# Sample attention by both key heads in one pass, sample state products of both halves side by side, small products queued behind the latest large one

## The chip, the cores and the metric

The kernel runs on one core of one Trainium2 chip. The metric is the time of one execution in device microseconds (us); before the change the median of three runs is 1966.09 us (1965.5 to 1967.4). PE is TensorE, DVE is VectorE, ACT is ScalarE, POOL is GpSimd, and SP is the engine whose queue issues nearly all DMA transfers here.

## The reference, cut to what matters

One decoder layer is applied to a prompt of 1024 tokens and to 8 running sequences with 8 new tokens each (64 sample tokens).

```python
x = x + 0.5 * rms_norm(swiglu(rms_norm(x, g1), ffn1_gu, ffn1_down), p1)
z = rms_norm(x, gm) @ w_in + b_in            # q, k, v | hq, hf, hi, hg
a = window_attention(q, k, v, sinks)         # prompt: 128-wide band; sample: 128 cached keys + 8 new ones
S, o = hgrn2(silu(hq), 1 - f, log f, hi, s0) # chunkwise; the sample starts from a given state
x = x + rms_norm(concat(rms_norm(a), gate(o)) @ w_out, pm)
x = x + 0.5 * rms_norm(swiglu(rms_norm(x, g2), ffn2_gu, ffn2_down), p2)
```

The sample attention has 2 key heads with 4 query heads each. For one sequence and one key head there are 32 query rows (4 heads by 8 tokens) against 136 keys. The sample recurrence has 4 heads; for each of the 8 sequences a state of 128x128 gets `S = decay * S + k^T v` over 8 tokens, and the output uses the old state.

## The kernel before, in words

All numbers are fp32. The large products are made of three fp32r products each: operands are split into a high part (ACT, L235) and a rest (DVE, L236), and `mm3` (L256) issues high by high, high by rest, rest by high (L258, L259, L260) into one PSUM bank. The tokens are three column groups of 320, 384 and 384: group 0 holds 256 prompt tokens and the 64 sample tokens, groups 1 and 2 hold prompt tokens. The program is the first FFN, the mixing part (projection `w_in_units`, attention, recurrence, projection `w_out_units`) and the second FFN. The down product of the first FFN for groups 1 and 2 is done in parts called `pair`, numbered by product: the parts 5, 3, 7 and 4 run after the projection of group 0 and before that of group 1. In a part each step takes two row blocks of the weight: the weight is loaded into `raw` (3 buffers), split into two of 8 `wsp` buffers, and the activations are loaded into `ar` (L927) and split into two halves of one `h` buffer; both share a ring of 8 buffers, from which the input of the next projection also takes its tiles. Three PSUM banks of a ring of four (`mm`) are added up by such a part, and `put` (L936) adds each to its sum with a DVE addition (L940).

The attention and the recurrence are small products that fill in. They are written as generators; `tick()` (L128) is called after every half or whole step of a large product and lets the generators advance at a rate (`pace`, L109) that is worked out from the steps still left (the second number in `ready`, L1469) and the tick at which they are due (`DUE`). The order on each engine is then set by the framework's scheduler, which may issue an instruction ahead of others that are written earlier if it thinks it is ready sooner. The small products use a second ring of four PSUM banks (`ax`).

The sample attention (`sample_attn`, L1344) goes over two halves `hb` of four sequences, and in each over the two key heads `g`: four score products (`ssc`, L1374) with 64 rows of the array and 32 columns each, mask and row maximum (DVE), exponential (ACT), two transposes (`spT`, L1391 and L1392), eight value products (`spv`, L1399 and L1403), scaling (DVE), store. There are four such rounds, one after another. The sample recurrence (`sample_hgrn`, L1418) goes over four heads `a`: value products `sav` (L1441, L1445) from the old state; the state is multiplied by its decay (POOL, L1447); then for each half `hf` of the sequences one state product `su` (L1451) with 32 rows of the array and 512 columns, and its addition to the state (DVE, L1453); the state is stored.

Of the kernel before, what the change touches and what calls it, by code (L numbers as in the profile page):

```python
# [14 lines left out]
ALU = mybir.AluOpType  # L15
# [3 lines left out]
P = 128  # L19
# [25 lines left out]
def tile_step(ctx: ExitStack, tc: tile.TileContext, A: dict, O: dict):  # L45
    nc = tc.nc
    V, S, G, PE = nc.vector, nc.scalar, nc.gpsimd, nc.tensor
# [15 lines left out]
    def axbank(s="ax"):  # L63
        return ps.tile([P, 512], F32, tag="ax", bufs=4, name=uid(s))
# [191 lines left out]
    def mm3(out, a, b, first, last, resume=False):  # L256

        PE.matmul(out, a[0], b[0], start=first, stop=False, skip_group_check=resume)  # L258
        PE.matmul(out, a[0], b[1], start=False, stop=False, skip_group_check=resume)  # L259
        return PE.matmul(out, a[1], b[0], start=False, stop=last, skip_group_check=resume)  # L260

    def hcol(h, k, w):
        return h[0][k // 4][:, k % 4, :w], h[1][k // 4][:, k % 4, :w]
# [740 lines left out]
    def mixing(tp, h):  # L1004
        w_in = A["w_in"]

        def t2(shape=(P, 512)):
            return tmp2("t2", shape)
# [335 lines left out]
        def sample_attn():  # L1344
            n = 0
            zq, kx, vn = Z[n]["q"], KX[n], VN[n]

            def cached(src, hb):
                t = tmp2("kv", (P, 4, P))
                nc.sync.dma_start(t, A[src][0, 4 * hb:4 * hb + 4].rearrange("b w g d -> w b (g d)"))  # L1350
# [12 lines left out]
            V.tensor_copy(keys[:, :, P:], kx[:, P + 256:P + 320].rearrange("p (b t) -> p b t", b=8))  # L1363
            qs = t2((P, 8, 4, 8))
            V.tensor_copy(qs.rearrange("p b m t -> p m b t"),
                          zq[:, :, 256:320].rearrange("p m (b t) -> p m b t", b=8))
            yield
            osc = dr.tile([4, P, 64], F32, name="osc")
            for hb in range(2):
                vc = cached("cache_v_win", hb)  # L1370
                for g in range(2):
                    bank = axbank("ssc")
                    for i in range(4):
                        PE.matmul(bank[32 * i:32 * i + 32, :136],  # L1374
                                  qs[64 * g:64 * g + 64, 4 * hb + i].rearrange("p m t -> p (m t)"),
                                  keys[64 * g:64 * g + 64, 4 * hb + i], start=True, stop=True)
                    p = t2((P, 136))
                    sm = small()
                    V.tensor_tensor_reduce(out=p, in0=bank[:, :136], in1=smask, op0=ALU.add, op1=ALU.max,
                                           scale=1.0, scalar=NEG, accum_out=sm[:, 0, 0:1])  # L1380
# [9 lines left out]
                    bank = axbank("spT")  # L1390
                    PE.transpose(bank[:, :P], p[:, :P], ident)  # L1391
                    PE.transpose(bank[:8, P:2 * P], p[:, P:136], ident)  # L1392
                    pT = t2((P, 2, P))
                    V.tensor_copy(pT[:, 0], bank[:, :P])
                    V.tensor_copy(pT[:8, 1], bank[:8, P:2 * P])
                    yield
                    ob = axbank("spv")
                    for i in range(4):
                        PE.matmul(ob[32 * i:32 * i + 32, :64], pT[:, 0, 32 * i:32 * i + 32],  # L1399
                                  vc[:, i, g * 64:g * 64 + 64], start=True, stop=False, skip_group_check=True)  # L1400
                    for i in range(4):
                        c = i * P + g * 64
                        PE.matmul(ob[32 * i:32 * i + 32, :64], pT[:8, 1, 32 * i:32 * i + 32],  # L1403
                                  vnb[hb][:8, c:c + 64], start=False, stop=True, skip_group_check=True)
                    o = t2((P, 64))
                    V.tensor_scalar(o, ob[:, :64], sm[:, 1, 2:3], None, op0=ALU.mult)
                    nc.sync.dma_start(osc[2 * g + hb], o)
                    yield
            o = t2()
            for b in range(8):  # L1410
                for g in range(2):
                    nc.sync.dma_start(
                        o[8 * b:8 * b + 8].rearrange("t (m g d) -> t g m d", m=4, g=2)[:, g],
                        osc[2 * g + b // 4, 32 * (b % 4):32 * (b % 4) + 32].rearrange("(m t) d -> t m d", m=4))
            yield
            yield from finish_attn(n, o, NS, slice(256, 320))

        def sample_hgrn():  # L1418
# [10 lines left out]
            for a in range(4):  # L1429
                st = big(F32, (P, 8, P))  # L1430
                nc.sync.dma_start(st, A["state_hgrn"][0][:, a].rearrange("b k v -> k b v"))
                qm = t2((P, 2, 4, 32))
                G.tensor_tensor(qm, Q[:, a, :r].rearrange("p (f t) -> p f t", f=2).unsqueeze(2).to_broadcast(
                    [P, 2, 4, 32]), own.unsqueeze(1).to_broadcast([P, 2, 4, 32]), op=ALU.mult)
                vb = t2((P, 4, P))
                V.tensor_tensor(vb[:r], z["v"][:r, 2, a * P:(a + 1) * P].unsqueeze(1).to_broadcast([r, 4, P]),
                                seqm.unsqueeze(2).to_broadcast([r, 4, P]), op=ALU.mult)
                yield
                sr = [slice(32 * hf, 32 * hf + 32) for hf in range(2)]
                for hf in range(2):  # L1440
                    PE.matmul(ob[sr[hf], a * P:(a + 1) * P], At[:r, a, sr[hf]], z["v"][:r, 2, a * P:(a + 1) * P],  # L1441
                              start=True, stop=False, skip_group_check=True)
                for b in range(4):
                    for hf in range(2):
                        PE.matmul(ob[sr[hf], a * P:(a + 1) * P], qm[:, hf, b], st[:, 4 * hf + b], start=False,  # L1445
                                  stop=b == 3, skip_group_check=True)
                G.tensor_tensor(st, st, D[:, a].unsqueeze(2).to_broadcast([P, 8, P]), op=ALU.mult)  # L1447
                yield
                for hf in range(2):
                    ub = axbank("su").rearrange("p (b t) -> p b t", b=4)  # L1450
                    PE.matmul(ub, kn[sr[hf], a], vb[sr[hf]], start=True, stop=True)  # L1451
# [318 lines left out]
```

## Time and profile before

| what | value |
|---|---|
| median of 3 runs | 1966.09 us (1965.5 to 1967.4) |
| the profiled execution, its own time | 1964.23 us |
| its span, first to last instruction | 1962.5 us |
| around the span | 1.7 us |
| PE / weight loads / DVE / ACT / POOL busy | 1944.9 / 1828.4 / 1368.5 / 932.2 / 209.1 us |
| granted PE clock, mean | 0.999 |
| DMA | 358.20 MB, 183 GB/s in the mean |

A row of the timeline gives the start of a group of instructions, its duration, engine, line, operation, the written and read tiles with the shape, and how many there are. Matmuls are pipelined, so that their durations overlap: what one costs is read from the starts of the instructions around it. An fp32 product that is not fp32r is run as two passes and counts as two in the trace. In a row of windows each engine has its busy time in that stretch, then the granted clock, the share of the DMA engines and the traffic.

### The profile page before, as it was taken

The numbers are of one execution on the slowest core, as the hardware profiler recorded it, in microseconds if no ns is written. First come the engines' busy times: TensorE is split into PE (matmuls) and PEld (weight loads), VectorE is DVE, ScalarE is ACT, GpSimd is POOL, SyncE is SP. The second block draws the span as 40 slices with busy tenths as digits, with TensorE's granted clock in tenths as the row PEclk, the third lists the DMA queues.
The fourth block names the chain that finished last, engine by engine and source line by source line (L and its number), as shares of the span: only waits on it lengthen the run. The fifth ranks groups of instructions, "written<-read, shape, count | busy, mean of one in ns | idle before, by whom it ended". The sixth has DMA issues, their size and how long they took to land.

```text
span 1962.5 us, 34190 instructions
## 1 busy us (share of the span) xinstructions
PE 1944.9 (99%) x13469; PEld 1828.4 (93%) x13469; DVE 1368.5 (70%) x2211; ACT 932.2 (48%) x1630; POOL 209.1 (11%) x213
## 2 busy tenths in 40 slices
PE   9999999999999999999999999999999999999998
PEld 8999999999998987788899898999999999999887
DVE  6976667777558666866667666745987877655666
ACT  6543333444455544744444565655544444444453
POOL 0000000000004012111232224001000000000202
PEclk9999999999999999999999999999999999999999
DMA  7543345556767645764434343556565545677874
GB/s 238 164 151 145 128 170 172 188 185 216 243 215 229 186 130 174 229 207 130 142 116 152 97 126 105 171 167 199 165 208 192 211 171 192 212 236 227 306 262 142
DMA packets 160396, 358.20 MB, mean 183 GB/s; under 512 B 16284, under 2 KB 59996, under 8 KB 160220
## 3 DMA queue, kind: packets, MB, share of 16 engines
q1 hardware_dynamic: 159228, 354.19, 54.5%
q8 instruction: 105, 1.72, 0.4%
q10 hardware_dynamic: 1008, 1.84, 0.3%
q14 instruction: 55, 0.45, 0.1%
HBM read 279.33 MB, written 77.63 MB: 182 GB/s over the span
## 4 chain that ended last, share of the span: by engine, by line
PE 94%; DVE 2%; DMA 2%; ACT 1%; issue 1%; POOL 0%; SPq 0%; DVEq 0%; POOLq 0%; ACTq 0%
PE mm L258 28%; PE mm L260 28%; PE mm L259 28%; DMA ar<-fa 1%; PE c L260 1%; PE c L258 1%; PE c L259 1%; PE sc L1154 1%; PE pv L1195 1%; PE lv L1228 1%; PE pT L1180 1%; DVE w L236 0%; PE mm L551 0%; PE av L1329 0%; DMA big<-in_x1T_dram 0%
## 5 line engine op out<-in xcount | busy, mean ns | idle before, releaser
L258 PE MATMUL mm<-h,wsph 128*128 128x320 f32 (+1 forms) x1296 | 416.3, 322 | 2.6 <-DVE sg L664 2.6
L259 PE MATMUL mm<-h,wsph 128*128 128x320 f32 (+1 forms) x1296 | 410.3, 317 | 0.0
L260 PE MATMUL mm<-h,wspl 128*128 128x320 f32 (+1 forms) x1296 | 408.9, 317 | 0.0
L236 DVE TENSOR_TENSOR wspl<-raw,wsph 128x1024 fp32r<-128x1024 f32 x200 | 250.7, 1254 | 148.9 <-ACT wsph L235 143.6
L235 ACT CAST wsph<-raw 128x1024 fp32r<-128x1024 f32 x200 | 208.9, 1047 | 296.0 <-PE mm L259 239.8
L235 ACT CAST w<-raw 128x512 fp32r<-128x512 f32 (+1 forms) x226 | 169.5, 754 | 239.7 <-PE mm L259 112.6
L236 DVE TENSOR_TENSOR w<-raw,w 128x512 fp32r<-128x512 f32 (+1 forms) x226 | 196.9, 875 | 85.4 <-ACT w L235 85.3
L258 PEld LDWEIGHTS mm<-h,wsph 128*128 128x128 f32 x1296 | 243.8, 188 | 10.2 <-issue 7.8
L259 PEld LDWEIGHTS mm<-h,wsph 128*128 128x128 f32 x1296 | 244.0, 188 | 1.7 <-issue 0.8
L260 PEld LDWEIGHTS mm<-h,wspl 128*128 128x128 f32 x1296 | 243.6, 188 | 1.4 <-issue 1.0
L258 PE MATMUL mm<-h,w 128*128 128x384 f32 x704 | 235.6, 335 | 0.0
L259 PE MATMUL mm<-h,w 128*128 128x384 f32 x704 | 235.6, 335 | 0.0
L260 PE MATMUL mm<-h,w 128*128 128x384 f32 x704 | 230.6, 335 | 0.0
L258 PE MATMUL mm<-w,h 128*128 128x512 f32 x462 | 181.5, 396 | 1.8 <-DVE big L940 1.3
L259 PE MATMUL mm<-w,h 128*128 128x512 f32 x462 | 180.3, 391 | 0.0
L260 PE MATMUL mm<-w,h 128*128 128x512 f32 x462 | 178.9, 391 | 0.4 <-DVE h L236 0.4
L229 POOL TENSOR_TENSOR sm<-sm,mhalf 128x3 f32<-128x3 f32 (+4 forms) x37 | 36.4, 987 | 1193.5 <-DVE sm L313 501.7
L258 PEld LDWEIGHTS mm<-h,w 128*128 128x128 f32 x704 | 132.2, 188 | 0.2 <-ACT big L754 0.2
L259 PEld LDWEIGHTS mm<-h,w 128*128 128x128 f32 x704 | 132.1, 188 | 0.0
L260 PEld LDWEIGHTS mm<-h,w 128*128 128x128 f32 x704 | 131.7, 188 | 0.0
L235 ACT CAST w<-t 128x512 fp32r<-128x512 f32 x176 | 106.8, 621 | 49.2 <-PE mm L260 46.0
L236 DVE TENSOR_TENSOR w<-t,w 128x512 fp32r<-128x512 f32 x176 | 119.0, 687 | 10.4 <-ACT w L235 10.4
(343 smaller groups left out, 3691.6 us busy)
## 6 DMA issues: line engine op xcount, KB each, us to landing
raw<-in_ffn_w_gu_dram SPq DMA_DIRECT2D x154, 512.0 KB
raw<-in_ffn_w_down_dram SPq DMA_DIRECT2D x74, 512.0 KB
raw<-in_w_in_dram SPq DMA_DIRECT2D x54, 512.0 KB
ar<-fa SPq DMA_DIRECT2D x70, 384.0 KB
big<-in_ffn_w_down_dram SPq DMA_DIRECT2D x88, 256.0 KB
fb<-big SPq DMA_DIRECT2D x44, 512.0 KB
raw<-fb SPq DMA_DIRECT2D x40, 512.0 KB
fa<-big SPq DMA_DIRECT2D x22, 768.0 KB
```

The lines of the kernel that those rows point to most:

```text
L229: G.tensor_tensor(y, x, mhalf[:y.shape[0], :y.shape[1]], op=ALU.pow)
L235: S.copy(hi, src)
L236: return (lo_eng or V).tensor_tensor(lo, src, hi.bitcast(F32), op=ALU.subtract)
L258: PE.matmul(out, a[0], b[0], start=first, stop=False, skip_group_check=resume)
L259: PE.matmul(out, a[0], b[1], start=False, stop=False, skip_group_check=resume)
L260: return PE.matmul(out, a[1], b[0], start=False, stop=last, skip_group_check=resume)
L1154: PE.matmul(banks[g][:, i * 256:i * 256 + wk], zq[64 * g:64 * g + 64, 2 * pr + i, b * P:(b + 1) * P], kx[64 * g:64 * g + 64, k0:k0 + wk], ...
L1180: PE.transpose(bank[:, (i * nk + kb) * P:(i * nk + kb + 1) * P], pt[g][:, i, kb * P:(kb + 1) * P], ident)
L1195: PE.matmul(ob[q0:q0 + 64, c:c + 64], pT[g][:, k1:k1 + 64], vn[:, vb, g * 64:g * 64 + 64], start=kb == 0, stop=kb == nk - 1)
L1228: PE.matmul(b4[ps_, j, a], x[:, a, cs], y[:, a, cs], start=True, stop=True)
```

## The change

There are three edits. In the sample attention both key heads are done in one round: the eight score products of a half are issued together (key head 1 first, key head 0 queued behind it on PE), both softmaxes follow, then the four transposes into one bank with two copies instead of four, then the sixteen value products into one bank, two scalings and two stores. In the sample recurrence both state products of a head are issued ahead of its value products (half 1 first, half 0 queued behind it), into two banks that are taken before; the additions to the state stay behind the decay. Last, what a `tick()` issues on PE is queued behind the large product that was written last, by an order constraint on PE alone which waits for nothing to finish. The numbers of steps in `ready` follow the generators: 11 for 17 and 10 for 14.

```diff
     def tick():
+        with tc.issue_after(latest[0].ins):
+            turn()
+
+    def turn():
         pace()
...
-        return PE.matmul(out, a[1], b[0], start=False, stop=last, skip_group_check=resume)
+        r = latest[0] = PE.matmul(out, a[1], b[0], start=False, stop=last, skip_group_check=resume)
+        return r
...
+                banks = [axbank("ssc") for _ in range(2)]
+                for g in (1, 0):
+                    with tc.issue_after(last) if g == 0 else nullcontext():
+                        for i in range(4):
+                            last = PE.matmul(banks[g][32 * i:32 * i + 32, :136],
+                                             qs[64 * g:64 * g + 64, 4 * hb + i].rearrange("p m t -> p (m t)"),
+                                             keys[64 * g:64 * g + 64, 4 * hb + i], start=True, stop=True).ins
...
+                ubs = [axbank("su").rearrange("p (b t) -> p b t", b=4) for _ in range(2)]
+                for hf in (1, 0):
+                    with tc.issue_after(last) if hf == 0 else nullcontext():
+                        last = PE.matmul(ubs[hf], kn[sr[hf], a], vb[sr[hf]], start=True, stop=True).ins
...
-                yield
                 for hf in range(2):
-                    ub = axbank("su").rearrange("p (b t) -> p b t", b=4)
-                    PE.matmul(ub, kn[sr[hf], a], vb[sr[hf]], start=True, stop=True)
                     sl = st[:, 4 * hf:4 * hf + 4]
-                    V.tensor_tensor(sl, sl, ub, op=ALU.add)
+                    V.tensor_tensor(sl, sl, ubs[hf], op=ALU.add)
...
-                    gens += [(sample_attn(), 17), (kv_out(0), 1)]
+                    gens += [(sample_attn(), 11), (kv_out(0), 1)]
...
-                    gens.append((sample_hgrn(), 14))
+                    gens.append((sample_hgrn(), 10))
```

The edits move instructions in the whole mixing part. On PE, before, in the projection of group 1, the two state products of the second head (`su`) come after two transposes of the sample attention (`spT`) and rows of the large product (`mm`), one row of which stands between the two:

```order
L1391 MATMUL spT_8898<-ident,t_1253_8796 128x128
L1392 MATMUL spT_8898<-ident,t_1253_8796 8x128
L258 MATMUL mm_8967<-h_8115,wsph_8963 128x384
L259 MATMUL mm_8967<-h_8117,wsph_8963 128x384
L1451 MATMUL su_8904<-t_1229_8697,m_1187_8458 128x512
L260 MATMUL mm_8967<-h_8115,wspl_8964 128x384
L1451 MATMUL su_8907<-t_1229_8697,m_1187_8458 128x512
```

The same engine after the change, at the third head, whose products stand as those of the fourth do:

```order
L264 MATMUL mm_9069<-h_8067,wspl_9066 128x384
L1459 MATMUL su_9119<-t_1288_9048,m_1207_8609 128x512
L1459 MATMUL su_9118<-t_1288_9048,m_1207_8609 128x512
L1461 MATMUL sav_8611<-big_6777,big_6474 32x128 x2
L1465 MATMUL sav_8611<-big_9044,t_1287_9046 32x128 x8
L262 MATMUL mm_9142<-h_8066,wsph_9138 128x384
```

The two state products of a head stand together, with the value products (`sav`) behind them. So it is at the third and the fourth head; at the first head the two stand together but apart from the value products, and at the second head one row of a large product still stands between them. In all, PE's order has 145 runs of small products between large ones, 164 before.

On SP, before, in the last part of the down product (product 4): loads of weights (`raw<-fb`) and of activations (`ar<-fa`) for its steps, loads for the next projection (`raw<-in_w_in_dram`), and two loads for the sample (`kv`, `big<-in_state_hgrn_dram`):

```order
L1350 DMA kv_8377<-in_cache_v_win_dram 128x4x128
L1431 DMA big_8461<-in_state_hgrn_dram 128x8x128
L915 DMA raw_8250<-fb_102 128x2x512
L915 DMA raw_8305<-fb_102 128x512
L927 DMA ar_8142<-fa_101 128x2x384
L242 DMA raw_8410<-in_w_in_dram 128x1024
L927 DMA ar_8207<-fa_101 128x2x384
```

The same place after the change, where ar_8093 holds the activations of the second step as ar_8142 does above:

```order
L922 DMA raw_8167<-fb_102 128x2x512
L391 DMA gb_8130<-in_norm_ffn_post_dram 128x512
L922 DMA raw_8210<-fb_102 128x2x512
L922 DMA raw_8259<-fb_102 128x512
L246 DMA raw_8366<-in_w_in_dram 128x1024
L934 DMA ar_8093<-fa_101 128x2x384
L246 DMA raw_8405<-in_w_in_dram 128x1024
```

The sample's two loads have gone from here to a later place, in the projection of group 1, and the first load for that projection now stands ahead of the activations of the second step, not behind them.

More of the change, by code (lines that the diff above doesn't have):

```diff
@@ L259, in mm3 @@
         PE.matmul(out, a[0], b[1], start=False, stop=False, skip_group_check=resume)
-        return PE.matmul(out, a[1], b[0], start=False, stop=last, skip_group_check=resume)
+        r = latest[0] = PE.matmul(out, a[1], b[0], start=False, stop=last, skip_group_check=resume)
+        return r
+    latest = [None]
     def hcol(h, k, w):
@@ L1370, in sample_attn @@
                 vc = cached("cache_v_win", hb)
-                for g in range(2):
[L1372 to L1376, printed above, removed]
+                banks = [axbank("ssc") for _ in range(2)]
[5 more added lines that the diff above has]
+                                             keys[64 * g:64 * g + 64, 4 * hb + i], start=True, stop=True).ins
+                ps_, sms = [], []
+                for g in range(2):
                     p = t2((P, 136))
                     sm = small()
-                    V.tensor_tensor_reduce(out=p, in0=bank[:, :136], in1=smask, op0=ALU.add, op1=ALU.max,
+                    V.tensor_tensor_reduce(out=p, in0=banks[g][:, :136], in1=smask, op0=ALU.add, op1=ALU.max,
                                            scale=1.0, scalar=NEG, accum_out=sm[:, 0, 0:1])
@@ L1388, in sample_attn @@
                     V.reciprocal(sm[:, 1, 2:3], sm[:, 1, 1:2])
-                    yield
[L1390 to L1397, printed above, removed]
+                    ps_.append(p)
+                    sms.append(sm)
+                yield
+                bank = axbank("spT")
+                for g in range(2):
+                    PE.transpose(bank[:, 2 * g * P:(2 * g + 1) * P], ps_[g][:, :P], ident)
+                    PE.transpose(bank[:8, (2 * g + 1) * P:(2 * g + 2) * P], ps_[g][:, P:136], ident)
+                pT = t2((P, 2, 2, P))
+                bank = bank.rearrange("p (g j t) -> p g j t", g=2, j=2)
+                V.tensor_copy(pT[:, :, 0], bank[:, :, 0])
+                V.tensor_copy(pT[:8, :, 1], bank[:8, :, 1])
+                yield
+                ob = axbank("spv")
+                for g in range(2):
                     for i in range(4):
-                        PE.matmul(ob[32 * i:32 * i + 32, :64], pT[:, 0, 32 * i:32 * i + 32],
+                        PE.matmul(ob[32 * i:32 * i + 32, g * 64:g * 64 + 64], pT[:, g, 0, 32 * i:32 * i + 32],
                                   vc[:, i, g * 64:g * 64 + 64], start=True, stop=False, skip_group_check=True)
@@ L1402, in sample_attn @@
                         c = i * P + g * 64
-                        PE.matmul(ob[32 * i:32 * i + 32, :64], pT[:8, 1, 32 * i:32 * i + 32],
+                        PE.matmul(ob[32 * i:32 * i + 32, g * 64:g * 64 + 64], pT[:8, g, 1, 32 * i:32 * i + 32],
                                   vnb[hb][:8, c:c + 64], start=False, stop=True, skip_group_check=True)
+                for g in range(2):
                     o = t2((P, 64))
-                    V.tensor_scalar(o, ob[:, :64], sm[:, 1, 2:3], None, op0=ALU.mult)
+                    V.tensor_scalar(o, ob[:, g * 64:g * 64 + 64], sms[g][:, 1, 2:3], None, op0=ALU.mult)
                     nc.sync.dma_start(osc[2 * g + hb], o)
-                    yield
+                yield
             o = t2()
```

1 line of the change is left out of this document (removed).

## The prediction

> **What bounds the kernel now.** I read the page's engines first, then the chain of waits, then the stretch in which the change moves things (from the last part of the down product, product 4, to the second half of the projection of group 1): by windows, by PE's waits there, and row by row. The lines are the span, the engines' busy time, and the chain's shares by engine.
>
> ```profile
> span 1962.5 us, 34190 instructions
> ...
> PE 1944.9 (99%) x13469; PEld 1828.4 (93%) x13469; DVE 1368.5 (70%) x2211; ACT 932.2 (48%) x1630; POOL 209.1 (11%) x213
> PE 94%; DVE 2%; DMA 2%; ACT 1%; issue 1%; POOL 0%; SPq 0%; DVEq 0%; POOLq 0%; ACTq 0%
> ```
>
> PE is busy for 99% of the span and carries 94% of the chain. So whatever PE no longer does is time saved, almost one for one; work that moves on DVE, ACT, POOL or SP costs nothing unless PE comes to wait for it. In the windows, start and end stand first, then length, the busy time of PE, weight loads, DVE, ACT and POOL, the granted clock, the DMA share and GB/s.
>
> ```profile
> 800.00:850.00 50.00, 47.08 (x279) 38.92 (x278) 40.30 (x68) 31.07 (x69) 8.64 (x7) 1.00 0.69 224
> 898.00:902.00 4.00, 4.00 (x17) 2.19 (x15) 2.92 (x5) 1.05 (x1) 0.00 (x0) 1.00 0.15 37
> 902.00:906.00 4.00, 4.00 (x15) 3.81 (x15) 0.69 (x1) 0.00 (x0) 0.00 (x0) 0.61 0.71 242
> ```
>
> Two kinds of loss besides the products themselves are seen. PE stands idle for 50 - 47.08 = 2.9 us in the first window, the end of product 4. And in the third PE is 4.00 of 4.00 us busy, but at a granted clock of 0.61: (1 - 0.61) x 4 = 1.6 us are lost. PE's waits from 740 to 960 us, with the total, the number and the longest, say what the idle time was for:
>
> ```profile
> PE kT L1324 <- DVE h L440: 1.7, 1, 1.7
> PE mm L258 <- DVE big L940: 1.3, 2, 0.9
> PE mm L260 <- DVE h L236: 0.4, 1, 0.4
> ```
>
> They end with DVE: inputs of the projection (L440), evictions of product 4 (L940) and the rest part of its activations (L236).
>
> **What a run of small products costs.** A matmul's duration overlaps the next, so I go by starts. Large products of 384 columns start 0.17 us apart. A state product alone, then both halves together, in the timeline:
>
> ```profile
> 866.53 0.34 PE L260 MATMUL mm<-h,wspl 128*128 128x384 f32 x1
> 866.80 1.12 PE L1451 MATMUL su<-t,m 32*128 32x512 f32 x2
> 867.85 0.44 PE L258 MATMUL mm<-h,wsph 128*128 128x384 f32 x1
> 868.13 0.34 PE L259 MATMUL mm<-h,wsph 128*128 128x384 f32 x1
> ...
> 917.34 0.33 PE L260 MATMUL mm<-h,wspl 128*128 128x384 f32 x1
> 917.60 1.13 PE L1451 MATMUL su<-t,m 32*128 32x512 f32 x4
> 918.66 0.44 PE L258 MATMUL mm<-h,wsph 128*128 128x384 f32 x1
> 918.93 0.33 PE L259 MATMUL mm<-h,wsph 128*128 128x384 f32 x1
> ```
>
> Alone: 0.27 instead of 0.17 before it (0.10 on entering), 1.05 to the next large product, and 0.28 instead of 0.17 after that one (0.11 on coming back): 1.26. The two together: 0.09 + 1.06 + 0.10 = 1.25. On different 32 rows of the array the second is free if it stands right behind the first. The value products of attention and recurrence:
>
> ```profile
> 856.65 0.33 PE L260 MATMUL mm<-h,wspl 128*128 128x384 f32 x1
> 856.82 0.34 PE L258 MATMUL mm<-h,wsph 128*128 128x384 f32 x1
> 857.09 0.32 PE L1399 MATMUL spv<-kv,t 128*32 128x64 f32 x8
> 857.34 0.31 PE L1403 MATMUL spv<-vnew,t 8*32 8x64 f32 x8
> 857.59 0.44 PE L259 MATMUL mm<-h,wsph 128*128 128x384 f32 x1
> 857.87 0.34 PE L260 MATMUL mm<-h,wspl 128*128 128x384 f32 x1
> 858.13 0.41 PE L1441 MATMUL sav<-big,big 64*32 64x128 f32 x4
> 858.47 1.07 PE L1445 MATMUL sav<-big,t 128*32 128x128 f32 x16
> 859.47 0.44 PE L258 MATMUL mm<-h,wsph 128*128 128x384 f32 x1
> 859.75 0.34 PE L259 MATMUL mm<-h,wsph 128*128 128x384 f32 x1
> ```
>
> By the same reading `spv` costs 0.10 + 0.50 + 0.11 = 0.71, and `sav` 0.09 + 1.34 + 0.11 = 1.54. The scores, between large rows of 512 columns (0.23 apart):
>
> ```profile
> 845.23 0.39 PE L259 MATMUL mm<-w,h 128*128 128x512 f32 x1
> 845.45 0.39 PE L260 MATMUL mm<-w,h 128*128 128x512 f32 x1
> 845.77 0.44 PE L1374 MATMUL ssc<-big,t 64*32 64x136 f32 x8
> 846.14 0.50 PE L258 MATMUL mm<-w,h 128*128 128x512 f32 x1
> 846.48 0.39 PE L259 MATMUL mm<-w,h 128*128 128x512 f32 x1
> ```
>
> That is 0.09 + 0.37 + 0.11 = 0.57. A transposition, which uses the whole array, starts 0.18 after the large product, so entering it costs nothing:
>
> ```profile
> 898.88 0.34 PE L260 MATMUL mm<-h,wspl 128*128 128x384 f32 x1
> 899.06 0.27 PE L1391 MATMUL spT<-ident,t 128*128 128x128 f32 x1
> ```
>
> **The change on PE.** State products: before, the order has four alone and two pairs, 4 x 1.26 + 2 x 1.25 = 7.5. After, the first head's pair stands by itself (1.25), the second's is still split by a large row (2 x 1.26 = 2.5), and the third's and fourth's stand right ahead of `sav`, which spares one entering and one coming back (1.25 - 0.20 = 1.05 each): 5.85. Saved 1.65. Scores: four runs, 4 x 0.57 = 2.28; after, two runs of both key heads, which are on different 64 rows: 2 x 0.57 = 1.14 if they run beside each other as the state products do, 2 x (0.57 + 0.37) = 1.88 if not. Saved 0.4 to 1.1; I take 0.7, since the outputs of both go to the same partitions, in two banks, as those of the state products do, but four column groups are in use at once. `spv`: 4 x 0.71 = 2.84 against 2 x (0.71 + 0.50) = 2.42; saved 0.4. Of the 19 runs that the order has fewer, these and the transposes explain 9. The other ten are neighbours from the prompt that came together when `tick` was bound to the latest large product. One such join is worth between nothing (a transposition at the seam, by the last row) and 0.2 (both ends spared), so 0 to 2.1; 0.3, near the lower end, as transposes and other products of the full array stand at most of these seams. Sum on PE: 1.65 + 0.7 + 0.4 + 0.3 = 3.0 saved, bounds 2.45 to 5.25. Nothing hides it: PE is the path.
>
> The Trainium skill (TensorEngine Tiling (Array Packing), Key Properties) says that changing the tiling mode drains TensorE. By this `sav` behind `su` would still drain, because its rows and columns differ, and the sum would be 2.6 rather than 3.0. No row here shows these two side by side; 2.6 lies in the range anyway.
>
> **The clock.** The dip from 902 to 906 us follows the second head's two state products with one large row between; the pair together at 917.60 has none behind it in the rows (0.17 to 0.27 apart). It needs, as these two cases read, more than about 1.1 us of products on a part of the array in a short stretch. After the change the second head is split just so again (another 1.6), and heads three and four have stretches of 1.06 + 1.34 = 2.4 us. The third and fourth may get a dip (up to 2 x 1.6 = 3.1 more) or the second may lose its own (1.6 less). I take no change.
>
> **Waits in product 4.** What SP issued there (duration of the issue, then what), and the two conversions that its step 2 waits for:
>
> ```profile
> 812.75 0.38 SPq L1350 DMA_DIRECT2D kv<-in_cache_v_win_dram  x1
> 813.48 0.38 SPq L1431 DMA_DIRECT2D big<-in_state_hgrn_dram  x1
> 814.48 3.55 SPq L915 DMA_DIRECT2D raw<-fb  x2
> 818.09 0.43 SPq L927 DMA_DIRECT2D ar<-fa  x1
> ...
> 823.02 0.83 ACT L235 CAST h<-ar 128x768 fp32r<-128x768 f32 x1 [0.93 <-DMA ar<-fa]
> ...
> 825.68 0.95 DVE L236 TENSOR_TENSOR h<-ar,h 128x768 fp32r<-128x768 f32 x1
> ```
>
> Step 2's activations are issued at 818.09, the cast waits 0.93 us for them, and the rest part ends at 826.63, when PE has just waited 0.4 us for it. Two things change. For the better: `kv` and the state load have left this place, and one conversion fewer stands ahead of the evictions on DVE, so that part of the 2.9 us can go. For the worse: `ar_8093` stands behind a weight load of the projection, which waits for a `raw` slot, and by the order that slot is freed one step later than the one that was needed before. A step is 2 row blocks x 3 token blocks x 3 products = 18 large rows of 512, 18 x 0.23 = 4.1 us (such rows start 0.22 to 0.23 apart at 845.23 above). DVE held the rest part back by 825.68 - 823.85 = 1.8 us after its cast, which takes up part of that. And fewer small products are left there for PE meanwhile: they went to group 1. So the bounds are -2.9 (all idle time gone) and +8.2 (steps 2 and 3 late by 4.1 each, all of it waited for); I take +0.5, near today's 0.4, since two opposite effects of like size meet.
>
> What else moves costs nothing while PE covers it. DVE has 70% and ACT 48% of the span, with counts nearly the same. The state's second load stands behind the store of the first head on SP; without its cover the value products would run later, as small work that large rows can stand in for. In the sample's chain the addition to the state now waits for POOL's decay with the `su` banks held; two of the four small banks are then taken for longer, which delays other small products, not PE.
>
> **Sum.** The profiled execution took 1964.23 us (span 1962.5 and 1.7 around it), 1.9 below the median of 1966.09. 1964.23 - 3.0 + 0 + 0.5 = 1961.7; on the median, 1966.09 - 2.5 = 1963.6.
>
> **Rivals.**
>
> *Waits go too.* The loads that left product 4 were the cause of its 2.9 us, and they go: -3.0 - 2.9 = -5.9, 1960.2. For it: two sample loads stand right ahead of the weights at 814.48. Against: the waits end with DVE, not with a DMA.
>
> *The dip goes.* If the clock falls for idle stretches and not for part-array products, the dip at 902 was a late answer to the 2.9 us of idle time in the first window, and goes where less idle time goes before: -2.5 - 1.6 = -4.1, 1962.0. Against: the idle time ended 75 us earlier, with clock 1.00 between. The Trainium skill (TensorE: Matmul & The Clock Gate, Part 1) states such a rule: half rate after an idle window of about 3.4 us, full rate while PE is busy. The row at 902 (busy 4.00 of 4.00, clock 0.61) speaks against it as it stands.
>
> *More dips.* Heads three and four get one each: -2.5 + 3.1 = +0.6, 1966.7.
>
> *The joins bring nothing.* The change may not do what it says: the second head is split still, and if `sav` behind `su`, the second key head's scores and the prompt's joins cost what they cost apart, only the first head's pair (2 x 1.26 - 1.25 = 1.27) and `spv` (0.4) are left of the saving: -1.7 + 0.5 = -1.2, 1964.9.
>
> *Slower: step 2's activations.* `ar_8093` and its successor come 4.1 us late each behind the projection's weight load, and PE, with less small work there, stands still for it: -3.0 + 8.2 = +5.2, 1971.3. It is slower from 6.9 us of waits on. For it: PE already waits for this h (0.4), so there is no slack; against it: DVE's 1.8 us.
>
> **How the numbers follow.** About 0.2%, 3.9 us, is what a measurement of this kernel can tell from no change. Forecast (1963.6) 0.31; waits go 0.24; dip goes 0.12; more dips 0.08; joins bring nothing 0.07; slower 0.18. Faster by over 0.2% (below 1962.2): 0.24 + 0.12 = 0.36. Within: 0.31 + 0.08 + 0.07 = 0.46. Slower: 0.18. The range goes from 1958.6 (waits and dip both gone, -7.5) to 1970.5 (most of the slower case: 7.4 of its 8.2 us).
>
> **What would show it.** Right: `su` with x4 at three of four heads, about 1.25 from large row to large row at the first; `ssc` x16 at under 0.6 between large rows; `spv` runs of about 1.2; PE busy less by about 3; idle time at product 4 within 1 us of 2.9. Wrong: a wait of several us for `ar<-fa` or `h L236` at product 4, more windows of clock under 0.7 after heads three and four, or runs of `ssc` that take twice as long. A PE that is idle for several us at a place not named here would make the prediction wrong altogether.

## The result and the profile after

| | before | after |
|---|---|---|
| median, runs side by side on one chip | 1965.13 us (12 runs, 1962.82 to 1967.4) | 1971.11 us (12 runs, 1967.1 to 1973.36) |
| ratio | | 1.0029 (95% interval 1.0021 to 1.0036) |
| the profiled execution | 1964.23 us | 1973.36 us |
| granted PE clock, mean of its span | 0.999 | 0.993 |

The change makes the kernel slower by 0.29%, 5 to 6 us. The profiled execution of the changed kernel is the longest of its twelve: its clock of 0.993 compares with 0.995 in their mean, so its trace shows more time at a low clock than most of them have. The page of the changed kernel has the same picture as before, with PE busy for more time, not less, and the same share of the chain:

```profile
span 1971.3 us, 34185 instructions
...
PE 1950.0 (99%) x13469; PEld 1834.9 (93%) x13469; DVE 1359.4 (69%) x2207; ACT 931.2 (47%) x1629; POOL 206.4 (10%) x213
...
PE 94%; DMA 2%; DVE 2%; ACT 1%; issue 1%; SPq 0%; DVEq 0%; POOLq 0%; POOL 0%; ACTq 0%
```

Where the time went is found by the large products: there are 10242 of them in both traces, so the start of the n-th can be compared. The difference of the starts (after less before, us), worked out from the two traces:

```
large product        0    500   3900   4400   4530   4548   4566   4629   4800   5100   6300  10200
starts before at     8     92    669    775    815    824    830    848    889    959   1236   1946
difference        -0.1    2.4    2.4    1.4   -0.7    1.5    7.8    9.6    3.2    9.8    8.8    8.8
```

The 2.4 us of the first 92 us are no part of the change: PE's three longest waits there are the same in both (2.6, 2.3 and 1.1 us), the clock falls behind them in some executions, and this difference was between -0.6 and 3.5 us over the profiles below. From 669 us to the end the changed kernel loses 6.4 us. It first gains 3.1 us up to the start of product 4 (4530, 814 us), and loses 10.3 us in product 4 (4530 to 4629). What follows goes up and down with small work that was moved, and ends 0.8 us lower.

In product 4, these are PE's waits from 800 to 850 us (before, in the same stretch: `kT` for DVE 1.7, `mm` for an eviction 0.9, `mm` for `h` 0.4), and the windows, again with the busy times of PE, weight loads, DVE, ACT and POOL, the granted clock and the DMA share:

```profile
PE mm L262 <- ACT h L239: 2.4, 2, 1.4
PE tr L442 <- DVE st L1344: 2.0, 1, 2.0
PE tr L442 <- DVE h L447: 1.1, 2, 0.6
PE tr L442 <- DVE big L1310: 1.0, 1, 1.0
```

```profile
800.00:850.00 50.00, 43.32 (x221) 34.22 (x220) 33.62 (x60) 28.21 (x63) 7.59 (x6) 0.86 0.52 166
816.00:820.00 4.00, 2.40 (x11) 1.66 (x9) 4.00 (x3) 3.91 (x17) 2.64 (x2) 1.00 0.23 66
820.00:824.00 4.00, 2.06 (x9) 1.31 (x9) 4.00 (x8) 1.74 (x3) 1.39 (x1) 0.59 0.70 228
824.00:828.00 4.00, 2.96 (x8) 2.07 (x7) 2.90 (x5) 1.31 (x2) 0.00 (x0) 0.50 0.61 194
828.00:832.00 4.00, 4.00 (x17) 3.49 (x16) 0.69 (x1) 0.59 (x1) 0.00 (x0) 0.63 0.12 41
...
916.00:920.00 4.00, 4.00 (x16) 3.92 (x16) 2.30 (x6) 1.83 (x3) 0.00 (x0) 0.57 0.93 288
```

PE is idle for 50 - 43.32 = 6.7 us (2.9 before), and the clock, which was 1.00 there before, is 0.86 over the window. It falls from 820 us on, when PE has been idle for 1.6 us of the four before. The three windows from 820 to 832 us lose (0.41 + 0.50 + 0.37) x 4 = 5.1 us, as about 10 us at half clock would, and in the last of them PE is busy all the time. Step 1 ends at 818 us, and step 2 starts at 825.38 (before: 823.91), behind three groups of transposes, the first of which is shown here with the cast of step 2's activations and PE's first product of step 2:

```profile
820.38 0.62 PE L442 MATMUL tr<-ident,big 128*128 128x128 f32 x3 [1.98 <-DVE st L1344]
...
824.50 0.83 ACT L239 CAST h<-ar 128x768 fp32r<-128x768 f32 x1 [1.40 <-DMA ar<-fa]
...
825.38 0.80 PE L262 MATMUL mm<-w,h 128*128 128x512 f32 x1 [1.04 <-ACT h L239]
```

Of the 4.6 us that PE waits there (2.0 + 0.6 + 1.0 + 1.0), 3.6 end with DVE, at transposes that PE's order sets ahead of step 2, and 1.0 with the cast, which had itself waited 1.40 us for its load. So step 2 could not start before its activations came, but they are not the whole of the wait. SP's rows show why the load is late:

```profile
809.39 8.44 SPq L922 DMA_DIRECT2D raw<-fb  x2
819.75 0.33 SPq L246 DMA_DIRECT2D raw<-in_w_in_dram  x1
820.17 0.39 SPq L934 DMA_DIRECT2D ar<-fa  x1
824.48 0.33 SPq L246 DMA_DIRECT2D raw<-in_w_in_dram  x1
824.91 0.39 SPq L934 DMA_DIRECT2D ar<-fa  x1
```

The second down weight is issued by 809.39 + 8.44 = 817.83. Then SP stands until 819.75 for a `raw` slot that the projection's weight needs, and only behind it, at 820.17, step 2's activations are issued; likewise at 824.48 and 824.91 for step 3. Before, the two loads of activations were issued at 818.09 and 822.89: each is 2 us later now, and PE was there earlier, because small work had left the place. Step 3 waits too, 1.4 us for a cast at 836.68, but that cast did not wait for its load, and the wait stays when the load comes 4 us earlier (the run with the activations as before, below).

The joined products themselves do what they were meant to. The first head's pair, then the third head's with its value products, then the scores of both key heads, then the value products of both:

```profile
887.95 0.34 PE L264 MATMUL mm<-h,wspl 128*128 128x384 f32 x1
888.22 1.13 PE L1459 MATMUL su<-t,m 32*128 32x512 f32 x4
889.28 0.44 PE L262 MATMUL mm<-h,wsph 128*128 128x384 f32 x1
...
929.56 0.34 PE L264 MATMUL mm<-h,wspl 128*128 128x384 f32 x1
929.83 1.13 PE L1459 MATMUL su<-t,m 32*128 32x512 f32 x4
930.89 0.41 PE L1461 MATMUL sav<-big,big 64*32 64x128 f32 x4
931.23 1.07 PE L1465 MATMUL sav<-big,t 128*32 128x128 f32 x16
932.22 0.44 PE L262 MATMUL mm<-h,wsph 128*128 128x384 f32 x1
932.50 0.34 PE L263 MATMUL mm<-h,wsph 128*128 128x384 f32 x1
```

```profile
882.51 0.34 PE L264 MATMUL mm<-h,wspl 128*128 128x384 f32 x1
882.78 0.46 PE L1382 MATMUL ssc<-big,t 64*32 64x136 f32 x16
883.17 0.45 PE L262 MATMUL mm<-h,wsph 128*128 128x384 f32 x1
...
926.29 0.34 PE L264 MATMUL mm<-h,wspl 128*128 128x384 f32 x1
926.56 0.32 PE L1414 MATMUL spv<-kv,t 128*32 128x64 f32 x8
926.80 0.31 PE L1418 MATMUL spv<-vnew,t 8*32 8x64 f32 x8
927.05 0.32 PE L1414 MATMUL spv<-kv,t 128*32 128x64 f32 x8
927.30 0.31 PE L1418 MATMUL spv<-vnew,t 8*32 8x64 f32 x8
927.54 0.44 PE L262 MATMUL mm<-h,wsph 128*128 128x384 f32 x1
```

The pair takes 1.06 us to the next large product, as one alone did. `su` and `sav` together cost 0.10 + 2.39 + 0.11 = 2.60 against 1.25 + 1.54 = 2.79 apart. Sixteen score products take 0.39 us where eight took 0.37. The value products take 0.98 us where eight and eight took 0.50.

### The profile page after: what moved, and what is told of

The parts are those of the page before. It is cut to its first block, busy times and chain, and to the rows that moved or that the text cites. A ratio compares the mean times of both kernels' runs of the same rounds, so it can differ in the third digit from the quotient of the medians.

```text
span 1971.3 us, 34185 instructions
## 1 busy us (share of the span) xinstructions
PE 1950.0 (99%) x13469; PEld 1834.9 (93%) x13469; DVE 1359.4 (69%) x2207; ACT 931.2 (47%) x1629; POOL 206.4 (10%) x213
## 4 chain that ended last, share of the span: by engine, by line
PE 94%; DMA 2%; DVE 2%; ACT 1%; issue 1%; SPq 0%; DVEq 0%; POOLq 0%; POOL 0%; ACTq 0%
PE mm L262 28%; PE mm L263 28%; PE mm L264 28%; DMA ar<-fa 1%; PE c L264 1%; PE c L262 1%; PE c L263 1%; PE pv L1202 1%; PE sc L1161 1%; PE pT L1187 1%; PE lv L1235 1%; DVE w L240 0%; DVE h L240 0%; ACT h L239 0%; PE av L1336 0%
```

## The experiments

Theory: the new step counts in `ready`, through the pace, give product 4 another order; in it SP issues weights of the projection ahead of activations, PE waits, and the clock falls behind the waits. Rival 1: the joined sample products, or clock dips behind them, cost the time. Rival 2: binding what `tick` issues to the latest large product costs it. Rival 3: it is the small work missing at product 4, or DVE's order there, whatever SP does. Each run is timed beside the kernel before on the same chip.

**The step counts alone**, on the kernel before:

```diff
-                    gens += [(sample_attn(), 17), (kv_out(0), 1)]
+                    gens += [(sample_attn(), 11), (kv_out(0), 1)]
-                    gens.append((sample_hgrn(), 14))
+                    gens.append((sample_hgrn(), 10))
```

> The kernel before with nothing but the two step counts changed (11 for 17, 10 for 14): no product is joined and nothing is bound to the latest large product. Theory (the loss comes from the end of the first FFN's last down product, product 4, whose order the counts set through the pace): the order there is that of the changed kernel, so PE idles 6 to 7 us between 800 and 850 us against 2.9 before, and the time is 4 to 9 us above the kernel before (about 1969 to 1974), more than the changed kernel's 5.7 if anything, since the joins' 3 us are not saved. Rival 1 (the joined sample products or clock dips behind them cost the time): as before, within 2 us of 1965. Rival 2 (binding tick's products to the latest large one costs it): as before, within 2 us of 1965.

Measured: 1987.33 us against 1965.2, ratio 1.0116 (1.0102 to 1.0129). PE's waits from 800 to 1000 us, then the window of product 4:

```profile
PE oT L1133 <- DVE t L1128: 6.6, 1, 6.6
PE tr L435 <- DVE st L1337: 2.9, 1, 2.9
PE tr L435 <- DVE big L1303: 1.0, 1, 1.0
PE mm L258 <- ACT h L235: 1.0, 1, 1.0
```

```profile
800.00:850.00 50.00, 43.76 (x250) 35.21 (x249) 35.89 (x66) 28.85 (x68) 9.03 (x7) 0.93 0.50 159
```

PE idles 6.2 us at product 4 and waits there as in the changed kernel, for DVE at transposes and for the cast, with no product joined and nothing bound. So the loss of product 4 comes with two numbers that no engine ever sees. The rest, 16 us more, lies between the large products 5100 and 5200, at the wait of 6.6 us for the end of the sample attention and the half clock behind it (0.53 in the mean from 972 to 990 us). There 17 steps were paced as if they were 11; that this makes it late is argued, not tried. The changed kernel hasn't that loss.

**The old counts, and the old counts without binding**, on the changed kernel:

```diff
-                    gens += [(sample_attn(), 11), (kv_out(0), 1)]
+                    gens += [(sample_attn(), 17), (kv_out(0), 1)]
-                    gens.append((sample_hgrn(), 10))
+                    gens.append((sample_hgrn(), 14))
```

> The changed kernel with the old step counts (17 and 14); all joins and the binding are kept. Theory: product 4 is ordered nearly as before (step 2's activations stand behind two weights of the down product and ahead of the projection's weights), PE idles 2 to 4 us between 800 and 850 us, and the joins' 3 us stay: 1961 to 1964, below the kernel before. Rival 1 (joined products, dips): 1970 to 1972 as the changed kernel. Rival 2 (binding): 1970 to 1972.

And in addition to it:

```diff
     def tick():
-        with tc.issue_after(latest[0].ins):
-            turn()
+        turn()
```

> The changed kernel with the old step counts and without the binding of tick's products to the latest large product; the joins in attention and recurrence are kept. Theory: SP's order at product 4 is that of the kernel before exactly, PE idles about 2.9 us between 800 and 850 us, 1961 to 1964. Rival 1: 1970 to 1972. Rival 2: 1961 to 1964, and 6 to 9 us below the run with old counts and binding.

Measured: 1970.2 us (ratio 1.0028, 1.0018 to 1.0039) with binding, 1965.14 us without (1.0005, 0.9996 to 1.0014). The first is a miss for the theory and lies in the range of both rivals, the second is half a miss: the loss is gone, but nothing is gained. With the old counts the binding brings other waits, which the changed kernel doesn't have or has shorter (`mm` for `big` is 0.5 us there). PE's two longest waits from 740 to 1000 us with old counts and binding:

```profile
PE mm L262 <- DVE big L947: 2.6, 3, 1.7
PE su L1459 <- DVE t L1452: 2.2, 1, 2.2
```

**The binding**, taken from the changed kernel (the edit above, with the new counts), and put alone into the kernel before:

> The changed kernel without the binding of tick's products to the latest large product; joins and new step counts are kept. The sample's joined runs and SP's order at product 4 (weight, activations of step 2, weight, activations of step 3) are the same as with it; only the prompt's small products move, and more of them stand behind step 2 (24 products of three kinds more). Theory (the counts set product 4's order, and SP's order makes PE wait): step 2 waits as in the changed kernel, 4 to 7 us of idle time between 800 and 850 us, 1968 to 1972. Rival (the binding is what costs, as the pair of runs with old counts suggests, 1970.2 against 1965.1): 1962 to 1966.

> The kernel before with nothing but the binding. At product 4 SP's order changes in one place: a second weight load of the projection stands ahead of step 3's activations. Theory (any weight load of the projection ahead of activations makes that step late): steps 2 and 3 lose 1 to 3 us, 1966 to 1969. Rival (the binding costs as much as the run with old counts suggests, 5 us, wherever it acts): 1970. Rival (the binding is neutral, and it was the joins' new order together with it that cost): 1964 to 1966.

Measured: 1969.75 us (1.0030, 1.0021 to 1.0039) and 1966.52 us (1.0006, 0.9997 to 1.0015). The four kernels with joined products, by counts and binding:

| | binding | none |
|---|---|---|
| new counts | 1971.11 | 1969.75 |
| old counts | 1970.2 | 1965.14 |

Without binding the new counts cost 4.6 us. With the new counts the binding costs 1.4 us, alone 1.5, and neither is told from none. With the old counts it costs 5.1 us, in the waits shown above; and with the binding the new counts cost only 0.9. So either edit alone is enough for a loss of about 5 us, in different places, and the table does not say by itself which of them acts in the changed kernel. In its trace the loss stands in product 4, as with the counts alone, and the run that mends SP's order there (below) keeps both edits.

**Each joined part alone**, on the kernel before with the old counts and no binding (the diff of the change, cut to `sample_attn` or to `sample_hgrn`):

> The kernel before with the joined sample attention alone, old step counts, no binding. Product 4 is ordered as before in all queues but one run of scores. Theory: scores and value products save 0.7 + 0.4 + 0.3 us and no wait comes in: 1963 to 1965, 0.3 to 2 us below the kernel before. Rival (each join's new order brings waits of its own in the projection of group 1, which eat its saving): 1965 to 1967.

> The kernel before with the joined sample recurrence alone, old step counts, no binding. Product 4 is ordered as before. Theory: at most three of the four heads have their state products together, 1 to 1.7 us saved, no new wait: 1963 to 1965. Rival (new waits in group 1's projection, since the state products now stand ahead of the value products and hold two banks): 1965 to 1968.

Measured: 1965.16 us (0.9998, 0.9990 to 1.0007) and 1964.53 us (0.9996, 0.9987 to 1.0005). Neither costs anything that can be seen, and rival 1 falls. A gain of 1 to 2 us is not told from none; in the two profiles the part from the large product 3900 to 6300 is 1.9 us shorter each.

**SP's order mended**, on the changed kernel. First, three weights behind step 2's activations:

```diff
-                nc.sync.dma_start(raw[:, :n], FA[:, k0:k0 + n, SLOT[m]])
+                f.acts[m, k0 // 2] = nc.sync.dma_start(raw[:, :n], FA[:, k0:k0 + n, SLOT[m]]).ins
...
-                wt = col_tile(c)
+                with tc.issue_after(f1.acts[4, 1]) if n == 1 and c in (Z_K, Z_V, 0) else nullcontext():
+                    wt = col_tile(c)
```

> The changed kernel with one order constraint more: the first three weight loads of group 1's projection are queued on SP behind the activation load of product 4's step 2. Theory in its narrow form (the load of step 2's activations stands behind a weight load that waits for a slot): that load is issued 2 us earlier, the waits ahead of step 2 (4.6 us, and half clock behind them) shrink by 2 to 3 us, step 3's activations stay late: 1967 to 1970. If all of the loss came from that one load: 1965 or below. Rival (the small work that left product 4 is what is missing, whatever SP does; joins or binding): 1970 to 1972.

Measured: 1971.22 us (1.0032, 1.0020 to 1.0045). The load is issued at 817.95, 2.2 us earlier, and the waits ahead of step 2 shrink from 4.6 to 1.9 us, but the three weights now stand ahead of step 3's activations, which are issued 4.6 us later than in the changed kernel (829.50). PE's longest wait from 800 to 850 us:

```profile
PE mm L262 <- ACT h L239: 4.5, 1, 4.5
```

The loss was only handed on to the next step. By its time alone this run speaks for rival 3 (1970 to 1972 expected, 1967 to 1970 by the theory); it is the place of the wait that speaks for SP's order. So the weights were spread as in the kernel before, behind the activations of steps 2, 4 and 5:

```diff
-                with tc.issue_after(f1.acts[4, 1]) if n == 1 and c in (Z_K, Z_V, 0) else nullcontext():
+                with tc.issue_after(f1.acts[4, {Z_K: 1, Z_V: 3, 0: 4}[c]]) if n == 1 and c in (Z_K, Z_V, 0) else nullcontext():
```

> The changed kernel with three order constraints on SP alone: the first three weight loads of group 1's projection are queued behind the activation loads of product 4's steps 2, 4 and 5, which gives SP at product 4 the order of the kernel before (activations, weight, two activations, weight, activations, weight). PE's joined sample runs and the new step counts stay. Theory (the counts move weight loads of the projection ahead of activations, PE waits for steps 2 and 3, and the clock falls behind the waits): the waits for activations at product 4 go, idle time between 800 and 850 us at 3 us or less, the granted clock over 0.97 there, 1962 to 1966. Rival (what is missing is small work, and DVE's order there is late whatever SP does): idle time 5 us or more and windows at half clock, 1968 to 1972.

Measured: 1965.13 us (1.0002, 0.9993 to 1.0010): the whole loss is gone. SP's rows, then PE's two longest waits and the window from 800 to 850 us:

```profile
818.35 0.39 SPq L936 DMA_DIRECT2D ar<-fa  x1
820.18 0.33 SPq L246 DMA_DIRECT2D raw<-in_w_in_dram  x1
820.61 4.41 SPq L936 DMA_DIRECT2D ar<-fa  x2
```

```profile
PE tr L442 <- DVE st L1347: 1.5, 1, 1.5
PE mm L262 <- ACT h L239: 1.5, 1, 1.5
```

```profile
800.00:850.00 50.00, 45.92 (x252) 36.89 (x251) 37.55 (x64) 29.44 (x65) 7.60 (x6) 0.97 0.57 185
```

Idle time is 4.1 us (I had expected 3 at most), and the clock is at 0.97 instead of 0.86. Step 2 starts at 822.58, 2.8 us earlier than in the changed kernel, and product 4 (large products 4530 to 4629) loses 3.9 us against the kernel before instead of 10.3. Joins, counts, binding and PE's sample runs are those of the changed kernel, so rivals 1 and 2 fall once more, and rival 3, as far as it says "whatever SP does", for most of the loss: what is left of the waits (4.1 against 2.9 us) may be its share. But the constraints on SP did not leave the other queues alone. The scheduler moved their work with the loads: on PE step 2's first products now stand ahead of the third group of transposes, and on ACT and DVE the conversions of its activations stand ahead of those of a weight. The run shows that the loss goes with SP's order and what the scheduler derives from it; it does not part the two. The wait for DVE at the first transposes (1.5 us) and the one at step 3 (1.5 us) are still there.

> As the run before it, but the three weight loads are queued behind all activation loads of product 4. Theory: no wait for activations; the projection's first weights come 5 us or more later, which costs nothing if they still are there at the end of product 4, and up to 4 us if not: 1962 to 1968. Rival (small work, DVE): 1968 to 1972.

With index 5, the last step, for all three weights: 1965.98 us (1.0002, 0.9993 to 1.0011). The weights come at 836.76 then, and PE does not wait for them.

**Counts in between**, joins without binding:

> Joins without binding, step counts between the old and the new ones (13 for attention, 12 for the recurrence). By the order, SP has step 2's activations ahead of the first weight load of the projection, and two activations ahead of the third. Theory: 1962 to 1966, with idle time below 4 us between 800 and 850 us. Rival (any counts below the old ones move small work out of product 4 and cost 4 us or more): 1968 to 1972.

> As the run with 13 and 12, but 14 for attention. By the order, the first weight load of the projection stands ahead of step 2's activations again, and PE has more small products (30 of two kinds) between step 1 and step 2. Theory: slower than the run with 13 and 12 by 2 us or more, 1966 to 1971. Rival (SP's order there is of no account): within 1.5 us of it.

Measured: 1968.21 us (1.0012, 1.0003 to 1.0021) and 1966.22 us (1.0008, 0.9999 to 1.0017). This pair says the opposite of what was expected: 14 and 12 is not the slower of the two, and 13 and 12 lies in the range of the rival (1968 to 1972). With 13 and 12, product 4 is as good as was forecast (PE busy 48.28 of 50 us, clock 1.00), but time is lost elsewhere; with 14 and 12, a weight ahead of step 2's activations costs little, with more small work at hand for PE. That SP's order costs only where PE has nothing else to do is how I read it; it was not tried. The 2 to 3 us of 13 and 12 stand in the clock's column of the next table. Its trace, of one of its faster executions (1965.55 us), has a wait of 2.0 us for an eviction, up to 789.70 us, and a clock of 0.67 from 788 to 792 us.

**The clock's share.** Every run lists its granted clock. The mean over the runs of time x (1 - clock) is what half clock took at most (idle time at a low clock counts too); the rest is the time at full clock:

| kernel (runs) | lost to the clock | rest |
|---|---|---|
| before (33) | 4.7 us | 1960.3 us |
| changed (12) | 10.2 us | 1960.6 us |
| changed, activations as before (11) | 5.9 us | 1959.4 us |
| changed, activations all first (11) | 5.4 us | 1960.1 us |
| changed, no binding (10) | 9.3 us | 1961.0 us |
| counts alone (4) | 19.9 us | 1967.7 us |
| joins, counts 13 and 12, no binding (11) | 7.7 us | 1960.1 us |

Of the 5.8 us between the means of changed and before, 5.5 stand in the clock's column. By this split, whose first column is an upper bound, the waits that were added and the products that were saved about cancel, and it is the clock behind the waits that makes the kernel slower.

## Why the prediction was wrong, point by point

- What bounds the kernel, and that PE's time counts one for one: right.
- The small products on PE, 3.0 us saved: right in every row that can be checked (the 0.3 us for the prompt's joins was not). First pair 1.25 forecast, 0.10 + 1.06 + 0.11 = 1.27 measured; `su` with `sav` 0.20 spared, 0.19 measured; `spv` 1.21 forecast, 0.10 + 0.98 + 0.11 = 1.19 measured. Only the scores were too dear: I took 0.7 us saved and it is 2.28 - 2 x 0.61 = 1.06, the second key head being free. The rule of the Trainium skill that I weighed (TensorEngine Tiling (Array Packing), Key Properties: a change of mode drains) holds inside the joined run: `su` takes 1.06 us to `sav` as to a large product. But the sum of 2.6 drawn from it did not follow, since the 0.19 are the entering and the coming back.
- The clock at the sample's products, no change: it came out so, but partly by luck. The second head's split pair has its dip again (0.57 from 916 to 920 us, with PE busy 4.00 of 4.00), and the joined stretches of heads three and four have none. But a pair split by one large product stands in eleven of the traces, and only three have a dip behind it (the kernel before, the changed kernel, and the changed kernel without binding). With the activations as before, for one, the pair starts at 907.98 and 909.41 us, and the clock is 1.00 from 908 to 916 us. So the 1.1 us of products that I had read from two cases do not decide it, and what does stays open. Nor is the rival by which the dip goes refuted: its condition, less idle time before, did not come about.
- **The step that failed is the term for the waits in product 4**, +0.5 us, "since two opposite effects of like size meet". They did not meet. The three waits of before are gone, but others came, and idle time rose from 2.9 to 6.7 us, that is by 3.8: 4.1 us at transposes that wait for DVE, which the prediction did not have, and 2.4 us for the casts of activations. The clock behind the waits took up to 5.5 us more (in the mean of the runs), and no term of the sum was for that. With SP's order mended the whole loss goes (1965.13 us, idle 4.1 us, clock 0.97). I had a part of the mechanism, as the rival of step 2's activations with two steps late and 1971.3 us, but gave it 0.18, because of DVE's 1.8 us of slack. That slack was no slack, and the rows of before could have told: there PE starts step 2 at 823.91, straight after the cast (823.02 + 0.83 = 823.85), and only later products of the step need what DVE makes. In the changed kernel it starts at 825.38, straight after the cast again (824.50 + 0.83 = 825.33). PE's first product of step 2 before:

```profile
823.91 0.49 PE L258 MATMUL mm<-w,h 128*128 128x512 f32 x1
```

- "4.1 us each" for the two loads was too much: they are 2.1 and 2.0 us later (820.17 against 818.09, 824.91 against 822.89). And only step 2 stood still for its load. That the rival's time came out nearly right (1971.3 against 1971.11) is luck: the clock, which it did not count, made up for it.
- The step counts were read as following the generators, with no cost of their own. They set the pace, and the pace sets who stands where in product 4; the counts alone brought nearly the same idle time (6.2 us).
- The range ended at 1970.5, with 7.4 of the rival's 8.2 us. With half clock behind the waits as a cost of its own it would have been wider.

## What to carry to other kernels

When a change alters a planner's numbers, compare the order at every place where an engine waits today, also far from the products that the change speaks of, and ask of each load that a slot's wait holds up what stands behind it on its queue. On a PE that is nearly always busy, price a wait with the clock behind it: here 3.8 us of additional waits cost the 3 us that the change had saved, and the clock up to 5.5 us besides. And an order that looks like a scheduling detail can be tried alone: three constraints on one queue gave the whole loss back. Compare the other queues' order in such a trial too, since the scheduler may move them with it, as it did here.

## What the runs showed of the hardware that was not expected

- A wait of about 2 us can be followed by half clock, and need not be. In the changed kernel PE waits for 2.0 us up to 820.38, is idle for 1.60 us of the window from 816 to 820 us, and the clock is near one half from 820 to 832 us. With the activations all first, waits of 1.8 and 0.7 us stand at the same place, PE is idle for 2.5 us of the same window, and the clock stays at 1.00. A wait of 2.6 us in the window from 24 to 28 us, the same in both kernels, is followed by a clock of 0.60 from 28 to 32 us in the changed kernel's trace and by 1.00 in that of the kernel before. The Trainium skill (TensorE: Matmul & The Clock Gate, Part 1) has half rate after an idle window of about 3.4 us. The trace has it begin behind a single wait of 2.0 us, and has it from 916 to 920 us with PE busy 4.00 of 4.00, so that by the measurement an idle window is not needed.
- DVE took longer while POOL ran. Two splits from 815.62 us took 4.11 us together, where one alone took 1.22, while POOL ran additions (busy 2.64 of the 4 us from 816):

```profile
804.45 1.22 DVE L240 TENSOR_TENSOR w<-raw,w 128x1024 fp32r<-128x1024 f32 x1
...
815.11 3.53 POOL L963 TENSOR_TENSOR big<-big,big 128x512 f32<-128x512 f32 x2 [1.07 <-DVE big L947]
...
815.62 4.11 DVE L240 TENSOR_TENSOR w<-raw,w 128x1024 fp32r<-128x1024 f32 x2
```

  These are 1.7 us more, and SP's wait for a slot ends with them, at 819.75. The Trainium skill (SBUF — State Buffer, SBUF: two separate sides) says that DVE and GpSimd lock a shared pair of ports for a whole instruction; the rows fit that, but no run here took POOL's additions away. It is not what the loss goes with: with the activations as before the two splits take 4.12 us, and the loss is gone.
